# A hybrid decoder layer on one core: chunk 0's q projection by blocks of 128 input features, with other priorities and filler shares

## The chip, the cores and the metric

One core of a Trainium2 chip runs one launch of the kernel. The metric is the device time in microseconds (us). Before the change, three timed runs gave 1933.70, 1939.51 and 1939.64 us (median 1939.51).

## What is computed

One layer on x of 2048 rows by 1024 features, all in float32. The reference, cut to what matters:

```python
h = rms_norm(x, attn_norm_g[l])
z = h @ w_in[l]
# columns of z: q 512, k 128, v 128, gate_b 512, gate_c 512, xc 512
q = rms_norm(q, q_norm_g[l])
k = rms_norm(k, k_norm_g[l])
y_attn = swa_sink_attention(q, k, v, sinks[l])     # 8 heads, 2 kv heads, window 128
y_conv = gate_b * short_conv(gate_c * xc, conv_w[l])
y = jnp.concatenate([rms_norm(y_attn, attn_out_g[l]),
                     rms_norm(y_conv, conv_out_g[l])], axis=-1)
x = x + y @ w_out[l]
hm = rms_norm(x, mlp_norm_g[l])
x = x + jnp.square(jax.nn.relu(hm @ w_up[l])) @ w_down[l]
```

## The kernel before

**Products.** TensorE multiplies in fp32r. An operand is split into a high part (a cast, on ScalarE, ACT) and a low part (operand minus high part, on VectorE, DVE), and one product becomes three: high by high, high by low, low by high (`mm3`, L266 to L268). So every weight that is loaded is split first; splits are L458/L459 in the first chunk and L245/L246 elsewhere.

**Stages.** The mixers (input projection, attention, convolution, output projection) run over four chunks of 512 rows, each four tiles of 128 rows. Weights of the input and output projections are split in chunk 0, stored to DRAM (`keep`), and loaded as parts in chunks 1 to 3. Then follows the MLP, whose up and down projections use seven products instead of eight for each 2 by 2 blocking, 2688 matmuls each (L1427 up, L1534 down), with operands in the pools `op_x` and `wop`.

**The first chunk.** x comes as four row tiles (`x0_0` to `x0_3`, the first in two halves), and the q, k, v weights in pieces of 256 columns: pieces 0 and 1 are q, piece 2 is k and v. TensorE starts with idle products (`spin`, L511), turns a row tile with eight transposes (L468), ACT and VectorE move it out of PSUM with the norm's gain (L474, L476, 128x128 at a time), and `product0` (L488) multiplies it by piece 0, row tile by row tile: 24 matmuls of 256 columns for each. This part is under `manual_schedule`: every engine runs it as written. Pieces 1 and 2 follow in `project_qkv(0)`. The row statistics come from `norm_stats` (a square with a running sum, L275); z is scaled by them at the end. The x tiles stay in memory as chunk 0's residual.

**What sets the order elsewhere.** A scheduler orders instructions by priority; `ahead(i)` reads an offset from `PRIO[stage][i]`. `FILL` gives, for each attention step of a chunk, how many steps of the other work go behind it (convolution, the convolution half of the output projection, and the next chunk's norm, transposes L294 and q, k, v projection). Each engine runs its queue strictly in order. [...]

**Lines that the steps touch.** L282 scales an x tile of the next chunk by its row statistics, L294 transposes it, L298 and L299 move it out of PSUM as high and low part; L768 and L769 sum squares of the attention output, behind ACT's L767; L892 adds an output projection to the residual. At the MLP's start L396 loads operand pieces of the normed rows, L411 loads weights of the up projection, L416 and L417 split them, L899 stores x1 on GpSimd's (POOL) queue, and L1111 are memsets of POOL that take the first buffers of the MLP's pools.

Of the kernel before, what the change touches and what calls it, by code (L numbers as in the profile page):

```python
# [7 lines left out]
F32 = mybir.dt.float32  # L8
# [71 lines left out]
SPIN = (5, 3)  # L80
SOON = 300
# [21 lines left out]
def hymba_layer(  # L103
# [99 lines left out]
    n_pieces = [0]  # L203
# [232 lines left out]
    x0 = [row("x1", f"x0_{t}", NT) for t in range(NT)]  # L436
    z0 = [zrow(f"z0_{t}") for t in range(NT)]
    raw0, raw1 = (raw_part(f"raw_qkv{pc}") for pc in range(2))
    hl0, hl1 = (high_low(0, f"w_qkv{pc}") for pc in range(2))
# [9 lines left out]
    def load_x0(t, cut=1):  # L449
        for i in range(cut):  # L450
            r = slice(i * D // cut, (i + 1) * D // cut)
            nc.sync.dma_start(x0[t][:, r], xf[t * P : (t + 1) * P, r])

    load_w0 = lambda i: nc.sync.dma_start(*cols256(wi, 0, pieces=2)(raw0)[i])

    def split0(i, raw, hl):
        r = slice(i * 512, (i + 1) * 512)
        nc.scalar.copy(hl[0][:, r], raw[:, r])  # L458
        nc.vector.tensor_tensor(hl[1][:, r], raw[:, r], hl[0][:, r].bitcast(F32), op=ALU.subtract)  # L459

    def moved(t, part):

        for i in range(2):
            kk = i * (KD // 2)
            if not part:
                pts[t, i] = bank("at", f"pt_a0_{t}_{i}")
                for j in range(4):
                    nc.tensor.transpose(pts[t, i][:, j * P : (j + 1) * P], x0[t][:, (kk + j) * P : (kk + j + 1) * P], ident)  # L468
            else:
                p3 = pts.pop((t, i)).rearrange("p (k t) -> p k t", k=4)  # L470
                dh, dl = (d[:, kk : kk + 4, t * P : (t + 1) * P] for d in h)
                for k in range(KD // 2):
                    g = g_in[kk + k]
                    nc.scalar.activation(dh[:, k], p3[:, k], AF.Copy, scale=g)  # L474
                for k in range(KD // 2):
                    nc.vector.scalar_tensor_tensor(  # L476
                        dl[:, k], p3[:, k], g_in[kk + k], dh[:, k].bitcast(F32), op0=ALU.mult, op1=ALU.subtract
                    )

    w0 = [w.rearrange("p (k c) -> p k c", k=KD) for w in hl0]  # L480

    def product0(t, i, ks=range(KD)):

        if (i, ks[0]) == (0, 0):
            pzs[t] = bank("mm", f"pz0_0_{t}")[:, :256]
        a, b = ((0, 0), (1, 0), (0, 1))[i]
        for k in ks:
            nc.tensor.matmul(  # L488
                pzs[t], h[a][:, k, t * P : (t + 1) * P], w0[b][:, k, :], start=i + k == 0, stop=i + k == KD + 1
            )  # L490

    def put_z(t):
        nc.scalar.activation(z0[t][:, :256], pzs[t], AF.Copy, scale=rs0[:, t : t + 1])

    pts, pzs = {}, {}

    with tc.manual_schedule(engines={ET.PE, ET.Activation, ET.DVE, ET.Pool, ET.SP}):
        nc.scalar.dma_start(g_rows, attn_norm_g[0].rearrange("(k p) -> k p", p=P))
        nc.scalar.activation(warm, mhalf[:, :1], AF.Square)
        load_x0(0, cut=2)  # L500
        load_w0(0)
        load_w0(1)
        for t in range(1, NT):
            load_x0(t)
        nc.sync.dma_start(*cols256(wi, 256)(raw1)[0])

        idle = bank("mm", "idle")[:, :P]

        def spin(n):
            for _ in range(n):  # L510
                nc.tensor.matmul(idle, ident, ident, start=True, stop=True)  # L511
# [5 lines left out]
        moved(0, 0)  # L517
        moved(0, 1)
        spin(SPIN[1])
        for i in range(4):  # L520
            split0(i, raw0, hl0)
            product0(0, 0, range(2 * i, 2 * i + 2))
            if i == 1:
                moved(1, 0)
        product0(0, 1)
        product0(0, 2)
        for t in range(1, NT):
            moved(t, 1)
            for i in range(4 if t + 1 == NT else 0):
                split0(i, raw1, hl1)  # L530
            norm_stats(x0[t - 1], f"a0_{t - 1}", rs0[:, t - 1 : t])
            if t > 1:
                put_z(t - 2)
            if t + 1 < NT:
                moved(t + 1, 0)
            for i in range(3):
                product0(t, i)
        norm_stats(x0[NT - 1], f"a0_{NT - 1}", rs0[:, NT - 1 : NT])
        put_z(NT - 2)
        put_z(NT - 1)  # L540
        rs0_in = nc.gpsimd.tensor_tensor(rs0_2, rs0, rs0, op=ALU.mult).ins


    with tc.tile_pool(name="mix_small", bufs=1) as mix_small, tc.tile_pool(name="mix", bufs=1) as mix:
# [10 lines left out]
        def project_qkv(c, h, z):  # L555

            z += z0 if not c else [zrow(f"z{c}_{t}") for t in range(NT)]
            if not c:
                keep(hl0, "qkv0")
            if not c:  # L560
                keep(hl1, "qkv1")
                for pc in range(1, 3):
                    hl = weights(cols256(wi, pc * 256), c, f"qkv{pc}") if pc > 1 else hl1
                    w4 = [w.rearrange("p (k c) -> p k c", k=KD) for w in hl]
                    for t in range(NT):
                        ps = bank("mm", f"pz{c}_{pc}_{t}")[:, :256]
                        hk = lambda s, k, t=t: h[s][:, k, t * P : (t + 1) * P]
                        for k in range(KD):
                            mm3(ps, lambda s, k=k: hk(s, k), lambda s, k=k: w4[s][:, k, :], k == 0, k == KD - 1)
                            if k % 2 and k < KD - 1:  # L570
                                yield
                        z_in.append(
                            nc.scalar.activation(
                                z[t][:, pc * 256 : (pc + 1) * 256], ps, AF.Copy, scale=rs0[:, t : t + 1]
                            ).ins
                        )
                        yield
                return

            both = []  # L580
            for half in range(2):
                hl = high_low(c, f"w_q{half}_{c}")
                for i in range(2):
                    for pc in range(2):
                        nc.sync.dma_start(
                            hl[i].bitcast(F32).rearrange("p (k c) -> p k c", k=KD // 2)[:, :, pc * 256 : (pc + 1) * 256],
                            parts_dram[f"qkv{pc}"][i].rearrange("p (k c) -> p k c", k=KD)[
                                :, half * (KD // 2) : (half + 1) * (KD // 2)
                            ],
                        )  # L590
                both.append([w.rearrange("p (k c) -> p k c", k=KD // 2) for w in hl])
# [20 lines left out]
        z_in = []  # L612
# [328 lines left out]
        def besides(c, before, h, yt, rc, x1, h_next, z_next):  # L941
# [105 lines left out]
        z = []  # L1047
        for _ in project_qkv(0, h, z):
            pass
# [10 lines left out]
        g_qk = const.tile([P, 2, DH], F32, name="g_qk")  # L1060
        nc.sync.dma_start(g_qk[:, 0, :], q_norm_g[0].partition_broadcast(P))
        nc.sync.dma_start(g_qk[:, 1, :], k_norm_g[0].partition_broadcast(P))
        with tc.issue_after(rs0_in):
            nc.gpsimd.tensor_scalar(g_qk[:, 0, :], g_qk[:, 0, :], DH**-0.5, None, op0=ALU.mult)
        sink = const.tile([P, HEADS], F32, name="sink")
        nc.sync.dma_start(sink, sinks[0].partition_broadcast(P))
# [3 lines left out]
        cw = const.tile([P, NCT, 3], F32, name="cw")  # L1070
        for t in range(3):
            nc.sync.dma_start(cw[:, :, t], conv_w[0][t].rearrange("(i p) -> p i", p=P))

        g_cols = const.tile([P, KD], F32, name="g_cols")
        nc.sync.dma_start(g_cols, mlp_norm_g[0].rearrange("(k p) -> p k", p=P))
        g_y = const.tile([P, 2, NCT], F32, name="g_y")
        for kv in range(KVH):
# [496 lines left out]
```

## Time and profile before

| | |
|---|---|
| timed runs | 1933.70, 1939.51, 1939.64 us |
| profiled execution | 1936.33 us, span 1934.6 us, mean granted clock 0.999 |
| TensorE (PE) busy | 1916.7 us, 99% of the span, 9025 matmuls |
| weight loads (PEld) | 1596.0 us, beside the matmuls |
| VectorE (DVE), ScalarE (ACT), GpSimd (POOL) busy | 1206.7, 837.7, 273.3 us |
| DMA | 412.25 MB, mean 213 GB/s over the span |
| first product of the q projection | at 8.57 us |
| end of chunk 0's q, k, v projection | at 48.80 us |
| up projection, from its long unbroken run | from 735 us |
| down projection | from 1321.43 us to the end |

The profile is of one execution, 1936.33 us by itself, and the span starts and ends with the first and last recorded instruction. In a timeline row the first number is the start, the second the length; "idle before <- releaser" says how long the engine had waited and what ended that. PE is TensorE's matmul side; a busy time of PE contains pipelined ends, so the pace of a row of matmuls is better read from the start of one group to the start of the next. In a windows row the last three numbers are the granted clock of TensorE (1.00 is full), the share of the 16 DMA engines in use and GB/s.

### The profile page before, as it was taken

The page shows a single profiled execution, that of the slowest core. Times are in us where ns is not written, and L with a number is a line of the kernel's source. Part 1 is how long each engine was busy: PE and PEld are TensorE (multiplying, and loading weights), DVE is VectorE, ACT ScalarE, POOL GpSimd, SP SyncE. Part 2 cuts the span into 40 slices and gives each one's busy share as a digit, 9 for nine tenths or more (in the row PEclk, how much of TensorE's full clock was granted, in tenths as well). Part 3 has the DMA queues.
Part 4 walks back from the last instruction along what each step waited for, and adds up shares of the span by engine and source line. Part 5 has one row for each costly group of instructions (what it writes and reads, how often), then busy time and mean ns, then how long its engine had stood idle before and what let it go on. Part 6 is the DMA issues. An engine that isn't in the chain of part 4 may idle for free.

```text
span 1934.6 us, 24806 instructions
## 1 busy us (share of the span) xinstructions
PE 1916.7 (99%) x9025; PEld 1596.0 (82%) x9025; DVE 1206.7 (62%) x1872; ACT 837.7 (43%) x1593; POOL 273.3 (14%) x473
## 2 busy tenths in 40 slices
PE   9999999999999999999999999999999999999999
PEld 9888888888888788888877888888888888888887
DVE  4885667447556768899878766666534334448541
ACT  6563445345344437445465554554422333232220
POOL 1112203312221112222201111101000000100000
PEclk9999999999999999999999999999999999999999
DMA  9774855464474787877665544437964457776631
GB/s 324 274 261 150 288 223 188 169 255 155 163 276 170 241 299 277 250 216 249 227 222 191 180 162 143 164 123 295 376 218 151 143 163 229 262 229 219 211 135 55
DMA packets 240634, 412.25 MB, mean 213 GB/s; under 512 B 51704, under 2 KB 147968, under 8 KB 228736
## 3 DMA queue, kind: packets, MB, share of 16 engines
q1 hardware_dynamic: 211824, 335.15, 51.3%
q0 software_dynamic: 15424, 51.40, 6.8%
q10 hardware_dynamic: 13264, 24.13, 3.3%
q8 instruction: 71, 1.16, 0.2%
q14 instruction: 51, 0.42, 0.1%
HBM read 284.78 MB, written 125.83 MB: 212 GB/s over the span
## 4 chain that ended last, share of the span: by engine, by line
PE 84%; issue 5%; DVE 4%; DMA 4%; ACT 2%; POOL 1%; SPq 1%; ACTq 0%; POOLq 0%; DVEq 0%
PE d L1534 31%; PE u L1427 23%; PE pout L266 2%; PE pout L268 2%; PE pout L267 2%; PE pz L266 2%; PE pz L267 2%; PE pz L268 2%; PE pc_c L266 2%; PE px_c L266 2%; PE px_c L267 2%; PE px_c L268 2%; PE pc_c L268 2%; PE pc_c L267 2%; PE psc_b L665 1%
## 5 line engine op out<-in xcount | busy, mean ns | idle before, releaser
L1427 PE MATMUL u<-op_x,wop 128*128 128x512 f32 x2688 | 612.5, 390 | 3.0 <-DVE wop L417 1.3
L1534 PE MATMUL d<-op_w,op_f 128*128 128x512 f32 x2688 | 609.4, 389 | 0.0
L1427 PEld LDWEIGHTS u<-op_x,wop 128*128 128x128 f32 x2688 | 503.7, 188 | 111.4 <-DVE wop L417 4.0
L1534 PEld LDWEIGHTS d<-op_w,op_f 128*128 128x128 f32 x2688 | 504.7, 188 | 104.6
L398 DVE TENSOR_TENSOR op_f<-op_f 128x1024 fp32r<-128x1024 f32 x112 | 136.9, 1225 | 237.8 <-ACT op_f L397 237.4
L397 ACT CAST op_f<-op_f 128x1024 fp32r<-128x1024 f32 x112 | 118.0, 1054 | 355.9 <-DMA op_f<-fop 343.7
L416 ACT CAST wop<-wu 128x512 fp32r<-128x512 f32 x156 | 96.4, 621 | 92.0 <-PE u L1427 87.7
L417 DVE TENSOR_TENSOR wop<-wu,wop 128x512 fp32r<-128x512 f32 x156 | 111.7, 717 | 34.1 <-ACT wop L416 19.0
L1163 POOL DMA_DIRECT2D fop<-s x96 | 52.3, 545 | 433.3 <-DVE s L1166 426.4
L1169 DVE TENSOR_TENSOR u<-u,u 128x512 f32<-128x512 f32 x128 | 87.8, 686 | 18.8 <-PE u L1427 18.8
L398 DVE TENSOR_TENSOR op_w<-raw,op_w 128x1024 fp32r<-128x1024 f32 x56 | 68.4, 1222 | 25.4 <-ACT op_w L397 25.4
L397 ACT CAST op_w<-raw 128x1024 fp32r<-128x1024 f32 x56 | 58.9, 1053 | 42.3 <-PE d L1534 20.1
L1175 ACT ACTIVATE u<-u 128x512 f32<-128x512 f32 x64 | 40.6, 634 | 51.7 <-DVE u L1169 50.0
L682 ACT ACTIVATE sc_b<-sc_b,ngm_b 128x128 f32<-128x128 f32 x128 | 49.9, 392 | 26.5 <-DVE ngm_b L679 26.5
L714 POOL TENSOR_SCALAR_AFFINE_SELECT pp_b<-pp_b 128x512 fp32r<-128x512 f32 x60 | 41.1, 697 | 116.9 <-ACT pp_b L707 63.4
L1376 POOL DMA_DIRECT2D wds<-raw x16 | 8.6, 535 | 333.8 <-DVE raw L1374 333.8
L416 ACT CAST wop<-wu_s 128x512 fp32r<-128x512 f32 x64 | 39.5, 621 | 35.6 <-PE u L1427 27.4
L266 PE MATMUL pout<-w_wo,yt_c 128*128 128x512 f32 x128 | 52.4, 410 | 0.0
L268 PE MATMUL pout<-w_wo,yt_c 128*128 128x512 f32 x128 | 51.9, 406 | 0.0
L267 PE MATMUL pout<-w_wo,yt_c 128*128 128x512 f32 x128 | 51.2, 400 | 0.0
L266 PE MATMUL pout<-w_wo,at_b 128*128 128x512 f32 x128 | 50.2, 395 | 0.2 <-DVE x L892 0.2
L267 PE MATMUL pout<-w_wo,at_b 128*128 128x512 f32 x128 | 50.0, 391 | 0.3 <-DVE w_wo L249 0.3
(255 smaller groups left out, 3132.7 us busy)
## 6 DMA issues: line engine op xcount, KB each, us to landing
op_f<-fop SPq DMA_DIRECT2D x112, 512.0 KB, 4.5
raw<-in_w_down_dram SPq DMA_DIRECT2D x72, 512.0 KB, 4.4
wu<-in_w_up_dram SPq DMA_DIRECT2D x128, 256.0 KB, 3.8
w_wo<-wo SPq DMA_DIRECT2D x24, 1024.0 KB, 6.8
fop<-s POOLq DMA_DIRECT2D x96, 256.0 KB, 2.7
fop<-u ACTq DMA_DIRECT2D x64, 256.0 KB, 2.3
op_x<-xop SPq DMA_DIRECT2D x28, 512.0 KB, 6.5
w_q<-qkv SPq DMA_DIRECT2D x24, 512.0 KB, 6.0
```

The source lines that it names most:

```text
L266: nc.tensor.matmul(ps, st(0), mv(0), start=first, stop=False)
L267: nc.tensor.matmul(ps, st(0), mv(1), start=False, stop=False)
L268: nc.tensor.matmul(ps, st(1), mv(0), start=False, stop=last)
L397: nc.scalar.copy(op[:, 0], raw)
L398: nc.vector.tensor_tensor(op[:, 1], raw, op[:, 0].bitcast(F32), op=ALU.subtract)
L416: splits.append(nc.scalar.copy(hi, blk).ins)
L417: nc.vector.tensor_tensor(lo, blk, hi.bitcast(F32), op=ALU.subtract)
L682: nc.scalar.activation(sc[:, hd, :], sc[:, hd, :], AF.Exp, bias=ngm[:, hd : hd + 1], accum_out=den[:, hd : hd + 1])
L1163: eng.dma_start(fop_dram[tb][ORDER_DOWN.index(i)][n // 2][:, n % 2], b)
L1169: return nc.vector.tensor_tensor(dst, ps, b, op=ALU.add).ins
L1427: nc.tensor.matmul(pt, wops[i][:, a, k, :], xops[tb, p][k // 2][:, b, k % 2, :], start=p not in GOES_ON and k + j == 0, stop=k + j == NB + ...
L1534: nc.tensor.matmul(ps[tb][j], fs[tb][:, a, k, j * P : (j + 1) * P], w[:, b, k, :], start=first and p not in GOES_ON and k + n == 0, stop=l ...
```

## The change

1. **Loads.** x of chunk 0 comes by blocks of 128 features: one tile [128, 4, 1024] in a pool of its own ("first"), blocks 0 and 1 singly (512 rows by 512 B), the others in pairs. The q weights come by the same blocks of 128 input features with all 512 columns, block 0 on ACT's queue. The small loads of gains, sinks and convolution weights go behind them.
2. **Loop.** For each block k: split of the weights, four transposes into one PSUM bank, one move of 128x512 on ACT and one on VectorE, 12 matmuls of 512 columns into four banks that stay open over the eight blocks. Transposes of block k+2 stand behind the products of block k. The k, v piece is loaded at k = 3 and multiplied after the loop, still in the order as written.
3. **Spin.** The second group of three idle products goes (`SPIN`).
4. **Residual and weights later.** Chunk 0's residual is loaded from x again, after its last z (four times 512 KB). The q parts are stored as two halves by features, so chunks 1 to 3 load them with four transfers of 1 MB instead of eight of 512 KB.
5. **Tables.** `PRIO`, `FILL` and `SOON` change, and a memset takes the first buffer of the MLP's pool "w".

The core of the diff:

```diff
-SPIN = (5, 3)
-SOON = 300
+SPIN = (5, 0)
+SOON = 330
-    (40, 0, 160, -10, 10, 0, 80, 10, -20, 30, 0, 300),
+    (40, 0, 160, -10, 10, 0, 10, 60, -20, 30, 0, 300),
...
-    n_pieces = [0]
+    n_pieces = [2]
...
+        def load_x0(k, n):
+            r = slice(k * P, (k + n) * P)
+            nc.sync.dma_start(x0[:, :, r], xf[:CH, r].rearrange("(t p) c -> p t c", p=P))
...
+        def turn(k):
+            pts[k] = bank("at", f"pt_a0_{k}")
+            for t in range(NT):
+                nc.tensor.transpose(pts[k][:, t * P : (t + 1) * P], x0[:, t, k * P : (k + 1) * P], ident)
...
+        def product0(k, order):
+            for i, t in order:
+                a, b = ((0, 0), (0, 1), (1, 0))[i]
+                nc.tensor.matmul(
+                    pzs[t],
+                    h[a][:, k, t * P : (t + 1) * P],
+                    hl0[k][:, b],
+                    start=k + i == 0,
+                    stop=k + i == KD + 1,
+                )
...
+        load_w0(nc.scalar, 0, 1)
         nc.scalar.activation(warm, mhalf[:, :1], AF.Square)
+        load_x0(0, 1)
+        load_x0(1, 1)
+        load_w0(nc.sync, 1, 1)
+        for k in range(2, KD, 2):
+            load_x0(k, 2)
+            load_w0(nc.sync, k, 2)
+        load_gains(0)
...
+        turn(0)
         spin(SPIN[1])
+        turn(1)
+        for k in range(KD):
+            split0(k)
+            moved(k)
+            if k == KH - 1:
+                raw = raw_part("raw_qkv2")
+                nc.sync.dma_start(*cols256(wi, AW)(raw)[0])
+                load_gains(1)
+            if k >= KH:
+                norm_stats(x0[:, k - KH], f"a0_{k - KH}", rs0[:, k - KH : k - KH + 1])
+            if k + 1 < KD:
+                product0(k, [(i, t) for i in range(3) for t in range(NT)])
+            else:
+                product0(k, [(i, t) for t in range(NT) for i in range(3)])
+            if k + 2 < KD:
+                turn(k + 2)
...
-            x1 += [] if c else x0
-            for t in range(NT if c else 0):
+            for t in range(NT):
                 r = (c * NT + t) * P
                 xr = row("x1", f"x1_{c}_{t}", NT)
-                nc.sync.dma_start(xr, xf[r : r + P, :])
+                with nullcontext() if c else tc.issue_after(z_in[-1]):
+                    nc.sync.dma_start(xr, xf[r : r + P, :])
...
-    for tag in ("f12", "s1", "s2", "s4", "u4", "f11"):
+    for tag in ("f12", "s1", "s2", "s4", "u4", "f11", "w"):
         nc.gpsimd.memset(piece(tag, f"{tag}_first")[:, :1], 0.0)
```

The order of TensorE's queue at the start of the program, before (`pt_a` are transposed x tiles, `idle` the idle products, `pz` the accumulators of q, `h_a` and `w_qkv` the split operands):

```order
L515 MATMUL pg<-ident,g_rows 128x8
L468 MATMUL pt_a_0_0_276<-ident,x_0_236 128x128 x4
L468 MATMUL pt_a_0_1_281<-ident,x_0_236 128x128 x4
L511 MATMUL idle<-ident 128x128 x3
L488 MATMUL pz_0_0_307<-w_qkv_0_246,h_a_250 128x256 x4
L468 MATMUL pt_a_1_0_314<-ident,x_1_237 128x128 x4
L468 MATMUL pt_a_1_1_319<-ident,x_1_237 128x128 x4
L488 MATMUL pz_0_0_307<-w_qkv_0_246,h_a_250 128x256 x4
```

The same place after the change, from the transposes of block 0 to the first product of the low weights:

```order
L496 MATMUL pt_a_0_290<-ident,x_265 128x128 x4
L496 MATMUL pt_a_1_295<-ident,x_265 128x128 x4
L508 MATMUL pz_0_0_300<-w_q_0_242,h_a_250 128x512
L508 MATMUL pz_0_1_301<-w_q_0_242,h_a_250 128x512
L508 MATMUL pz_0_2_302<-w_q_0_242,h_a_250 128x512
L508 MATMUL pz_0_3_303<-w_q_0_242,h_a_250 128x512
L508 MATMUL pz_0_0_300<-w_q_0_242,h_a_250 128x512
```

The idle products between transposes and products are gone, and the first eight transposes are two blocks of 128 features of all four row tiles instead of one row tile.

VectorE's queue near the end of chunk 0's attention, before (`xt_a_2` is x tile 2 of chunk 1, `o_b` the attention output of the last row tile but one, `x_0` the residual):

```order
L768 TENSOR_TENSOR o_b_1712<-o_b_1712 128x256 [waits Activation_49]
L648 TENSOR_TENSOR kw<-ptk_b_1729,kw 64x128
L769 TENSOR_TENSOR o_b_1712<-o_b_1712 128x128 [waits DVE_49]
L299 TENSOR_TENSOR h_h_1562<-pt_a_1_4_1751,h_h_1561 128x4x128
L892 SCALAR_TENSOR_TENSOR x_0_236<-pout_1_1_0_1804,rc_808,x_0_236 128x512 [waits PE_49]
L282 SCALAR_TENSOR_TENSOR xt_a_2_1687<-xt_a_2_1687,rs_a_2_1692,g_attn 128x1024 [waits DMAHW5_49,Pool_49]
```

And after the change (lines L768 and L892 have become L782 and L906):

```order
L282 SCALAR_TENSOR_TENSOR xt_a_2_1549<-xt_a_2_1549,rs_a_2_1554,g_attn 128x1024 [waits DMAHW6_49,Pool_49]
L906 SCALAR_TENSOR_TENSOR x_0_0_1415<-pout_1_1_0_1666,rc_662,x_0_0_1415 128x512 [waits PE_49]
L780 TENSOR_TENSOR at_b_1579<-o_b_1574,at_b_1579 128x512 [waits Activation_49]
L690 COPY_PREDICATED sc_b_1687<-later,psc_b_0_1688 128x128 [waits Activation_49]
L299 TENSOR_TENSOR h_h_1424<-pt_a_2_0_1639,h_h_1423 128x4x128 [waits Activation_49]
L782 TENSOR_TENSOR o_b_1574<-o_b_1574 128x256 [waits Activation_49]
```

The scale of the x tile has moved from behind the sums of the attention output to ahead of them.

SP's queue at the start of the MLP, before (`op_x` are operand pieces, `wu` weights of the up projection):

```order
L396 DMA op_x_2_1_6973<-xop_1_77 128x1024 [waits DMAHW5_49,PE_49]
L411 DMA wu_12_6987<-in_w_up_dram 128x4x128 [waits DMAHW6_49]
L396 DMA op_x_6_0_6977<-xop_2_78 128x1024 [waits DMAHW7_49,Pool_49]
L396 DMA op_x_6_1_6981<-xop_2_78 128x1024 [waits DMAHW0_49,PE_49]
L411 DMA wu_12_6989<-in_w_up_dram 128x4x128 [waits DMAHW1_49]
```

And after the change (`xt_m_0` is the first row tile of x1 of the last chunk, stored by POOL's queue before, which is the semaphore DMASW1):

```order
L396 DMA op_x_2_1_6825<-xop_1_77 128x1024 [waits DMAHW3_49,PE_49]
L1219 DMA xt_m_0_7369<-x_dram 128x1024 [waits DMAHW4_49,DMASW1_49]
L396 DMA op_x_6_0_6829<-xop_2_78 128x1024 [waits DMAHW5_49,Pool_49]
L396 DMA op_x_6_1_6833<-xop_2_78 128x1024 [waits DMAHW7_49,DMAHW6_49,DVE_49]
L411 DMA wu_12_6839<-in_w_up_dram 128x4x128
```

The load of x1 stood 26 rows further down before, behind the weights of the up projection; it now stands ahead of `op_x_6_0` and of the first `wu_12`.

More of the change, by code (lines that the diff above doesn't have):

```diff
@@ L432, in begin_mlp @@
             wops[i] = split_up(b, f"{m}_{p}")
-    x0 = [row("x1", f"x0_{t}", NT) for t in range(NT)]
     z0 = [zrow(f"z0_{t}") for t in range(NT)]
-    raw0, raw1 = (raw_part(f"raw_qkv{pc}") for pc in range(2))
-    hl0, hl1 = (high_low(0, f"w_qkv{pc}") for pc in range(2))
+    raw0 = [raw_part(f"raw_q{half}") for half in range(2)]
+    hl0 = [wop_pool.tile([P, 2, AW], F32R, tag="wop", name=f"w_q0_{k}", bufs=NWOP) for k in range(NWOP)]
+    hl0 += [pool.tile([P, 2, AW], F32R, tag="at", name=f"w_q0_{k}", bufs=NAT) for k in range(NWOP, KD)]
     h = parts(pool, "h", "a0")
@@ L447, in hymba_layer @@
     g_in = [g_in_all[:, k : k + 1] for k in range(KD)]
[L449 to L478, printed above, removed]
@@ new lines, in first_chunk @@
+        for t in range(NT):
+            ps = bank("at", f"pz0_1_{t}")[:, :256]
+            hk = lambda s, k, t=t: h[s][:, k, t * P : (t + 1) * P]
+            for k in range(KD):
+                mm3(ps, lambda s, k=k: hk(s, k), lambda s, k=k: w4[s][:, k, :], k == 0, k == KD - 1)
+            z_in.append(nc.scalar.activation(z0[t][:, AW:], ps, AF.Copy, scale=rs0[:, t : t + 1]).ins)
+        return rs0_in, hl
+    z_in = []
+    with tc.tile_pool(name="first", bufs=1) as first:
+        with tc.manual_schedule(engines={ET.PE, ET.Activation, ET.DVE, ET.Pool, ET.SP}):
+            rs0_in, w_qkv2 = first_chunk(first)
@@ L544, in hymba_layer @@
+    keep(w_qkv2, "qkv2")
+    for half in range(2):
+        d = dram.tile([2, P, 2048], F32, name=f"q{half}")
+        parts_dram[f"q{half}"] = [d[i] for i in range(2)]
+        with tc.high_priority(offset=-LATER):
+            for k in range(KH):
+                nc.sync.dma_start(
+                    d[:, :, k * AW : (k + 1) * AW].rearrange("i p c -> p i c"), hl0[half * KH + k].bitcast(F32)
+                )
     with tc.tile_pool(name="mix_small", bufs=1) as mix_small, tc.tile_pool(name="mix", bufs=1) as mix:
@@ L555, in project_qkv @@
         def project_qkv(c, h, z):
[L557 to L591, printed above, removed]
+            z += [zrow(f"z{c}_{t}") for t in range(NT)]
+            both = [[by_k(w) for w in weights(None, c, f"q{half}")] for half in range(2)]
             w4 = [w.rearrange("p (k c) -> p k c", k=KD) for w in weights(None, c, "qkv2")]
```

111 lines of the change are left out of this document (49 added, 62 removed), and 10 rows, old and new, of tables (FILL, PRIO).

## The prediction

> **What bounds the kernel now.** I read the page first, then the waits of the matmul engine over the whole span, then the first 50 us as a timeline and as windows. The page has busy shares, and the chain that ended last:
>
> ```profile
> PE 1916.7 (99%) x9025; PEld 1596.0 (82%) x9025; DVE 1206.7 (62%) x1872; ACT 837.7 (43%) x1593; POOL 273.3 (14%) x473
> PE 84%; issue 5%; DVE 4%; DMA 4%; ACT 2%; POOL 1%; SPq 1%; ACTq 0%; POOLq 0%; DVEq 0%
> 1321.43 609.29 PE d L1534 x2688
> ```
>
> The last row is from the chain in order of time: 2688 products in 609.29 us, 226.7 ns each for 512 columns, without a gap. TensorE is the bound, and it is 18 us (1934.6 - 1916.7) short of never idle. So the change can win in three ways: fewer or wider matmuls, a full clock earlier, or less idling. The three longest waits of TensorE (total, times, longest, in us) are short each:
>
> ```profile
> PE pt_a L294 <- DVE h_h L299: 1.7, 5, 0.5
> PE idle L511 <- POOL ident L170: 1.6, 1, 1.6
> PE u L1427 <- DVE wop L417: 1.3, 3, 0.5
> ```
>
> The place with most to win is the start. TensorE's timeline there (start, length, idle before and what ended it), and then windows with the busy time of PE, PEld, DVE, ACT and POOL, the granted clock and the DMA share:
>
> ```profile
> 1.58 2.50 PE L511 MATMUL idle<-ident 128*128 128x128 f32 x10 [1.58 <-POOL ident L170]
> ...
> 4.22 1.97 PE L468 MATMUL pt_a<-ident,x 128*128 128x128 f32 x8
> 5.98 1.49 PE L511 MATMUL idle<-ident 128*128 128x128 f32 x6
> 8.57 1.02 PE L488 MATMUL pz<-w_qkv,h_a 128*128 128x256 f32 x4 [1.10 <-ACT w_qkv L458]
> 10.55 1.39 PE L468 MATMUL pt_a<-ident,x 128*128 128x128 f32 x8 [0.96 <-DMA x<-in_x_dram]
> ...
> 19.14 1.04 PE L468 MATMUL pt_a<-ident,x 128*128 128x128 f32 x8
> 19.93 5.99 PE L488 MATMUL pz<-w_qkv,h_a 128*128 128x256 f32 x48
> ```
>
> ```profile
> 0.00:7.79 7.79, 5.88 (x25) 5.34 (x25) 1.41 (x6) 3.67 (x10) 1.78 (x18) 1.00 0.68 222
> 7.79:11.20 3.41, 1.65 (x10) 1.25 (x11) 3.41 (x8) 2.28 (x4) 0.00 (x0) 1.00 1.03 411
> 11.20:14.61 3.41, 3.41 (x19) 3.41 (x17) 2.17 (x9) 3.22 (x10) 0.06 (x1) 0.50 1.05 315
> 14.61:25.76 11.15, 11.15 (x97) 11.15 (x96) 6.73 (x20) 9.57 (x27) 2.05 (x6) 1.00 0.72 203
> 25.76:48.80 23.04, 23.04 (x195) 23.04 (x193) 9.50 (x18) 12.05 (x26) 5.87 (x12) 1.00 1.04 408
> ```
>
> Three things are to be seen. The first product runs at 8.57 us, after waiting for split weights. Eight transposes take 1.76 us from 4.22 to 5.98, but 0.79 from 19.14 to 19.93 (0.10 each): TensorE is at half pace early, though the clock column says 1.00 there (I trust the pace). And the thin stretch 7.79 to 11.20 (1.65 us busy of 3.41) is followed by one with a granted clock of 0.50. The last row is the 192 products of the two later pieces, 120 ns each; the projection of chunk 0 ends at 48.80.
>
> **The change, part by part.**
>
> *q projection by feature blocks.* 192 products of 256 columns become 96 of 512: 192 x 0.120 = 23.0 us against 96 x 0.2267 = 21.8, so -1.3 us. The transposes stay 32. When does the first product run? The loads, splits and moves now:
>
> ```profile
> 0.80 0.59 ACTq L498 DMA_DIRECT2D g_rows<-in_attn_norm_g_dram  x1
> 0.81 0.86 SPq L452 DMA_DIRECT2D x<-in_x_dram  x2
> x<-in_x_dram SPq DMA_DIRECT2D x2, 256.0 KB, 3.2
> raw_qkv<-in_w_in_dram SPq DMA_DIRECT2D x2, 512.0 KB, 6.6
> L458 ACT CAST w_qkv<-raw_qkv 128x512 fp32r<-128x512 f32 x8 | 4.5, 645 | 0.6 <-DMA raw_qkv<-in_w_in_dram 0.6
> L1059 ACT COPY rs_row<-pr 128x512 f32<-128x512 f32 x1 | 0.6, 578 | 0.0
> L459 DVE TENSOR_TENSOR w_qkv<-raw_qkv,w_qkv 128x512 fp32r<-128x512 f32 x8 | 5.1, 687 | 0.0
> ```
>
> x block 0 is 256 KB like the half tile now loaded first, so it lands near 4.1. The weights of block 0 are 256 KB too (512 KB took 6.6), issued on ACT's queue near 1.4: they land between 4.6 and 6.0. Then ACT copies (0.57 unloaded, 0.645 mean) and moves (0.58, as the copy from PSUM): first product at 6.0 to 7.8, and I take 7.0. VectorE needs 0.69 for each of its two, 1.4 per block; ACT 1.2, from block 4 on 1.1 more for a norm's square. TensorE needs 12 x 0.227 + 4 x 0.10 = 3.1 us per block, so both engines keep ahead. So do loads: a block is 512 KB, and even the 222 GB/s of the first window bring one in 2.4 us. This is the cover of everything else in the loop; gone, each us of a late block is a us of time.
>
> From the first product: 21.8 + 24 x 0.10 = 24.2 us at full pace. The three idle products dropped (six rows of 0.21 at half pace) filled a wait, so they save nothing themselves, but they held TensorE busy before 7.79. Without them the stretch 4.37 to 7.79 has 8 transposes (1.76) and 0.8 of products: 2.5 of 3.41 us. That lies between the stretch that kept half clock behind it (1.65) and the one from 1.58 to 4.37 (2.8 busy, still half pace after it). So I take the half pace until 11.20, with (11.2 - 7.0)/2 = 2.1 us lost; the stretch after that is full in any case, since no wait for x tiles is left in it. The q part then ends at 7.0 + 24.2 + 2.1 = 33.3. The k and v piece is 96 x 0.12 = 11.5 us, to 44.8: **-4.0 us** against 48.80. The bounds: full pace from 7.79 gives 43.1 (-5.7); a first product at 7.8 with half pace to 14.61 gives 46.9 (-1.9).
>
> [...]
>
> *Other loads.* The k, v weights are issued inside the loop and land long before 33. The residual x of chunk 0 is loaded a second time: 2 MB at the rate of the next row is 6 us of all DMA engines, in a stretch that is nearly full:
>
> ```profile
> 60.00:80.00 20.00, 20.00 (x100) 16.69 (x99) 17.38 (x41) 11.97 (x38) 4.19 (x7) 1.00 0.95 327
> ```
>
> TensorE is never idle there, and the sums that read the residual come only at the out projection, after 120. I cost it at 0, and up to +2 if it pushes the x tiles of chunk 1, whose last wait is known (chain, then VectorE and TensorE):
>
> ```profile
> 137.61 5.93 DMA xt_a<-in_x_dram
> 145.34 0.43 DVE L768 TENSOR_TENSOR o_b<-o_b 128x256 f32<-128x256 f32 x1 [1.15 <-ACT o_b L767]
> 147.69 1.27 DVE L282 SCALAR_TENSOR_TENSOR xt_a<-xt_a,rs_a,g_attn 128x1024 f32<-128x1024 f32 x1
> 149.02 0.65 PE L294 MATMUL pt_a<-ident,xt_a 128*128 128x128 f32 x4 [1.13 <-DVE xt_a L282]
> ```
>
> Half the q weight loads (4 of 1 MB for 8 of 512 KB) frees four SP issues per chunk, and SP has time: 0.
>
> *Mixers' priorities.* In the order of VectorE, the scale of x tile 2 of chunk 1 (L282, at 147.69) now stands ahead of the attention sums that held it up (L768): TensorE's wait of 1.13 and the one of 0.6 around it should go, -1.9; one earlier wait grows as transposes come closer together, +1.0. Net **-0.9**. The other chunks' waits are of the same size and shift both ways; I take 0, with -3 to +2 as ends (all of the listed waits, or two of them more).
>
> *MLP's start.* A load of the x1 rows (xt_m) now stands on SP ahead of the operand pieces and first weights of the up projection, and waits for a store that POOL issues:
>
> ```profile
> 696.68 13.99 SPq L396 DMA_DIRECT2D op_x<-xop  x2
> 706.44 0.64 POOL L899 DMA_DIRECT2D x_dram<-x  x1 [14.70 <-DVE x L892]
> 720.87 0.19 POOL L1111 MEMSET s_first<- 128x1 f32 x3 [6.10 <-DMA x_dram<-x]
> 712.88 21.47 PE L1427 MATMUL u<-op_x,wop 128*128 128x512 f32 x94
> x_dram<-x SPq DMA_DIRECT2D x12, 512.0 KB, 3.5
> wu<-in_w_up_dram SPq DMA_DIRECT2D x128, 256.0 KB, 3.8
> ```
>
> SP stands still until 710.7 now as well. Such a store takes 3.5 us as a median, and the last one held POOL's memset for 6.1; at 5 for this one, SP goes on at 711.4; two operand loads and the weights are issued by 712.7, land at 716.5, are split by 717.9 (1.34 by the page's L416 and L417), and are wanted at 717.9, 22 products behind 712.88. I take **+0.5**, from 0 to +9. The memset for the dummy waits in POOL's row where others wait: 0.
>
> Sum: -4.0 - 0.9 + 0.5 = -4.4. The first wait (1.6 for the identity) stays. The profiled execution took 1936.33, so 1931.9; the three timed runs are 1933.70, 1939.51 and 1939.64 (with the profiled one 1937.3 in the mean), so the same program scatters by 3 us around my base. I put the forecast at **1932.0**.
>
> **The rivals.**
>
> *The clock is free early and the mixers gain.* For it: the phase of the stretches is not shown to be fixed, and the start of before had full pace from 7.79. Start -5.7, mixers -0.9 - 3: 1936.3 - 9.6 + 0.5 = 1927.
>
> *The start gains nothing that lasts.* SP and DMA are nearly full from 25 to 80, so TensorE could wait at the x tiles of chunk 1 for what it won before: with the DMA landing at 143.5 as the fixed point, 1936. Against it: TensorE waits little there, and the tile is loaded behind buffers that come free earlier too.
>
> *Slower: the up projection's first weights come late.* The mechanism is the blocked SP row above. Its point is a store that lands after 711.4: beyond it each us is a us of time. If the slot is freed only with the last store (720.8, by POOL's memset row), the weights are issued at 722.1, landed at 725.9 and split at 727.3, against 717.9: +9.4, so 1931.4 + 9.4 = 1941. For it: SP runs strictly in order, and the row before had let those loads out at 696. Against it: the row names the first of four stores.
>
> *The loads starve the blocks,* because x now comes in pieces of 512 B to 1 KB. It needs blocks slower than 3.1 us (170 GB/s); at 5 us each the q part ends at 47: start +9.7, 1946. The 222 GB/s speak against it.
>
> **How the numbers follow.** Forecast 0.50, early clock with mixers 0.25, nothing that lasts 0.11, late weights 0.11, starved blocks 0.03. A measurement of this kernel can tell 0.3% (5.8 us) from no change: below 1930.5 is faster. The early clock case lies there (0.25), and of the forecast's own spread (1928 to 1936, by the bounds of the start and the other terms) two fifths of its 0.50, so 0.20: together 0.45 faster. Slower by 0.3% needs 1942: 0.03 and half of the late weights, 0.09 with some of the forecast's own upper end. The rest, 0.46, is within. The range from 1924 (both early cases with all waits) to 1940 leaves out most of the two slow cases.
>
> **What would show it.** Right: first product near 7.0, k and v done near 45, half pace ended at 11.2; no wait of TensorE at x tile 2 near 145; no wait longer than 1 us at the up projection's second operand. Wrong: waits on DMA or ACT inside the eight blocks, a second thin stretch with clock 0.50, or TensorE idle for several us behind SP near 715.

## The result, and the profile after

The changed kernel takes 1933.67 us (median of 21 runs, 1930.90 to 1936.15) against 1937.02 (21 runs, 1931.94 to 1941.29) before: ratio 0.9982, 95% interval 0.9976 to 0.9988, so 3.4 us less. The forecast was 1932.0. The profiled execution took 1934.50 us, 1.8 less than the one before. The page (busy, and shares of the chain) still has TensorE as the bound:

```profile
PE 1913.2 (99%) x8923; PEld 1589.5 (82%) x8923; DVE 1204.1 (62%) x1848; ACT 830.8 (43%) x1565; POOL 275.9 (14%) x474
PE 93%; DMA 2%; DVE 2%; issue 1%; POOL 1%; ACT 1%; SPq 0%; ACTq 0%; POOLq 0%; DVEq 0%
```

TensorE's timeline at the start, then its first work behind the k and v piece (`pr`), and the first transpose of the normed q (`ptq_b`, which reads `z`):

```profile
4.22 1.91 PE L496 MATMUL pt_a<-ident,x 128*128 128x128 f32 x8
6.43 3.02 PE L508 MATMUL pz<-w_q,h_a 128*128 128x512 f32 x12 [0.29 <-ACT h_a L500]
9.29 0.60 PE L496 MATMUL pt_a<-ident,x 128*128 128x128 f32 x4
...
42.81 0.60 PE L1070 MATMUL pr<-ident,rs_row 128*128 128x128 f32 x4
...
47.11 0.45 PE L652 MATMUL ptq_b<-ident,z 128*128 128x128 f32 x1 [3.01 <-DVE z L641]
```

The first product runs at 6.43, and its 12 products take 2.86 us to the next transposes: full pace from the first one (the next blocks take the same 2.86). The projection ends at 42.81 against 48.80, so 6.0 us are won. The last row shows 3.0 of them lost again in one wait. TensorE's longest waits in the whole span (total, times, longest; before, none was over 1.7 in total) are for split weights of the up projection (`wop`), for `z`, and for x1 rows loaded back for the MLP's norm (`xt_m`):

```profile
PE u L1421 <- ACT wop L416: 4.6, 1, 4.6
PE ptq_b L652 <- DVE z L641: 3.0, 1, 3.0
PE pt_m L308 <- DVE xt_m L282: 2.6, 3, 1.8
```

The windows around the two new waits (busy PE, PEld, DVE, ACT, POOL, granted clock, DMA share, GB/s):

```profile
42.81:47.11 4.30, 1.30 (x9) 0.84 (x8) 2.02 (x5) 1.44 (x4) 2.67 (x3) 0.95 1.01 350
47.11:50.53 3.42, 3.42 (x12) 2.61 (x13) 1.19 (x5) 2.54 (x6) 2.29 (x2) 0.57 1.02 413
50.53:53.94 3.41, 3.41 (x17) 2.80 (x16) 2.31 (x4) 2.98 (x9) 0.90 (x2) 1.00 1.02 425
714.46:719.04 4.58, 0.16 (x1) 0.00 (x0) 2.45 (x2) 1.85 (x3) 0.00 (x0) 1.00 1.07 379
719.20:722.60 3.40, 3.40 (x8) 2.68 (x9) 2.78 (x5) 2.60 (x5) 0.00 (x0) 0.51 1.15 345
```

Each wait is paid twice: behind the empty stretch comes one of 3.4 us with a granted clock of 0.57 or 0.51, which costs about 1.5 and 1.7 us more. So the wait at 47 costs 4.6 us, the one at 714 about 6.3.

Where the 6.0 us stay is read from marks that stand in both traces. From the chain and the timelines, before and after: the scores of the second row tile (16 matmuls) 65.67 and 64.25, those of chunk 2 390.16 and 386.96, the first store of x1 in the last chunk 706.44 and 703.02, the down projection's start 1321.43 and 1319.52. The lead is 6.0 us at 43, 1.4 at 65, 3.2 at 390, 3.4 at 705 and 1.9 at the end. The matmuls behind the projection of chunk 0 are the same in both kernels; taken where equally much of that work is still to come, the lead is the same at the last four marks.

### The profile page after: what moved, and what is told of

It is laid out like the page before. It is cut to its first block, busy times and chain, and to the rows that moved or that the text cites. A ratio compares the mean times of both kernels' runs of the same rounds, so it can differ in the third digit from the quotient of the medians.

```text
span 1932.8 us, 24559 instructions
## 1 busy us (share of the span) xinstructions
PE 1913.2 (99%) x8923; PEld 1589.5 (82%) x8923; DVE 1204.1 (62%) x1848; ACT 830.8 (43%) x1565; POOL 275.9 (14%) x474
## 4 chain that ended last, share of the span: by engine, by line
PE 93%; DMA 2%; DVE 2%; issue 1%; POOL 1%; ACT 1%; SPq 0%; ACTq 0%; POOLq 0%; DVEq 0%
PE d L1528 32%; PE u L1421 31%; PE pout L266 2%; PE pout L268 2%; PE pout L267 2%; PE pz L266 2%; PE pz L267 2%; PE pz L268 2%; PE psc_b L679 2%; PE pc_c L266 2%; PE px_c L266 2%; PE px_c L267 2%; PE pc_c L267 2%; PE pc_c L268 2%; PE px_c L268 2%; PE pb_c L267 1%
## 5 line engine op out<-in xcount | busy, mean ns | idle before, releaser
L417 DVE TENSOR_TENSOR wop<-wu_s,wop 128x512 fp32r<-128x512 f32 x64 | 45.0, 702 | 12.4 <-ACT wop L416 12.1
L266 PE MATMUL pout<-w_wo,at_b 128*128 128x512 f32 x128 | 50.2, 395 | 0.0
```

Of the source, the lines that this page charges most:

```text
L266: nc.tensor.matmul(ps, st(0), mv(0), start=first, stop=False)
L417: nc.vector.tensor_tensor(lo, blk, hi.bitcast(F32), op=ALU.subtract)
```

## The experiments

Ratios are to the kernel before, timed on the same chip; the changed kernel has 0.9982. The intervals in brackets are about 0.0009 either way, 1.7 us. "The dummy" is the memset that takes the first buffer of the MLP's pool "w".

### 1. Without the dummy

```diff
-    for tag in ("f12", "s1", "s2", "s4", "u4", "f11", "w"):
+    for tag in ("f12", "s1", "s2", "s4", "u4", "f11"):
```

> The changed kernel without the memset on the first buffer of the MLP's pool w. In SP's order the load of x1 (xt_m) then stands 30 rows further down again, and the first weights of the up projection ahead of it. Theory (the dummy moves the load, and that makes TensorE's wait of 4.6 us at L1421): that wait goes. If the dummy has no other effect, 4 us less than the changed kernel (1929.5); if it is also what removed the 4.2 us of small stalls that the kernel before has between 735 and 1100, those come back and the time stays at 1933 to 1934. Rival (the weights land late because the DMA engines are full): the wait stays at 4 us or more, wherever the load stands.

Measured: 1936.80 us, ratio 1.0003 (0.9994 to 1.0012): the whole gain is gone. The wait is 3.0 instead of 4.6 and begins 1.7 us later, and the stalls between 735 and 1100 are back. That stretch as a window, of the kernel before, the changed one, and this one:

```profile
735.00:1100.00 365.00, 363.12 (x1592) 298.24 (x1593) 311.39 (x449) 200.25 (x331) 73.85 (x104) 1.00 0.70 224
```
```profile
735.00:1100.00 365.00, 365.00 (x1612) 302.24 (x1611) 312.76 (x451) 203.02 (x334) 79.05 (x106) 1.00 0.71 225
```
```profile
735.00:1100.00 365.00, 363.78 (x1596) 298.43 (x1596) 310.65 (x450) 199.15 (x331) 74.43 (x105) 1.00 0.70 224
```

TensorE is never idle there in the changed kernel; without the dummy it loses 16 matmuls' time in the window, and the kernel before lost 20. Most of the stalls stand between 1000 and 1040. Neither theory was whole: the dummy does move the load of x1, and its stalls do come back, but the wait at the MLP's start does not go either. Without the dummy the first weights stand ahead on SP (SyncE, whose queue issues these loads), and wait there themselves for a buffer that TensorE's output projection frees (a wait of 14.7 us on SP): SP issues them at 708.6.

```profile
708.62 0.38 SPq L411 DMA_DIRECT2D wu<-in_w_up_dram  x1
```

So beside the changed kernel the dummy is worth 4 us.

### 2. The small loads on GpSimd

```diff
-                load_gains(1)
...
         rs0_in = nc.gpsimd.tensor_tensor(rs0_2, rs0, rs0, op=ALU.mult).ins
+        load_gains(1)       # its seven loads by nc.gpsimd
```

> The changed kernel with its seven small loads (cw, g_cols, g_y) issued by GpSimd after the row statistics instead of by SP inside the loop. Theory (TensorE's wait of 3.0 us for z at 47 us comes from ACT's split of w_wc, which stands ahead of z and waits for a load that SP issued only at 29.3 behind the small loads): the load of w_wc is issued near 26, lands near 35, the wait of 3.0 goes, and with it the slow pace of the 3.4 us behind it (1.5): 4 to 4.5 us less than the changed kernel, near 1929.5. Rival (the DMA engines are full between 25 and 45, so the weights land near 38 in any order): no change, 1933.5.

Measured: 1931.43 us, ratio 0.9980 (0.9971 to 0.9989), not to be told from the changed kernel. The profiled execution shows no wait for z, but its projection ended 1.6 us later, at 44.39, which hides it. The load of w_wc was issued at 27.36 and the split began at 36.11, against 29.32 and 38.47.

### 3. Both edits

Edits 1 and 2 in one kernel.

> Both edits in one kernel: small loads on GpSimd, and no dummy. Theory: the two effects add, 1925 to 1929.5 (the lower end if the dummy costs its whole 4.6 us). Rivals: 1933.5 if neither place is what it seems.

Measured: 1933.15 us, ratio 0.9981 (0.9972 to 0.9990). Its rows judge edit 2 better, since the projection ended at 42.91 as in the changed kernel:

```profile
25.87 0.37 SPq L239 DMA_DIRECT2D raw_wc<-in_w_in_dram  x1
```
```profile
37.55 2.19 ACT L245 CAST w_wc<-raw_wc 128x512 fp32r<-128x512 f32 x4 [5.21 <-DMA raw_wc<-in_w_in_dram]
```
```profile
46.20 0.45 PE L652 MATMUL ptq_b<-ident,z 128*128 128x128 f32 x1 [1.99 <-DVE z L641]
```

Issued 3.5 us earlier, w_wc lands 0.9 us earlier, and TensorE still waits 2.0 us for z. That is the rival of experiment 2 for the larger part, though the two rows are not of one load alone: with edit 2, SP also issues the first residual load of x (512 KB) ahead of w_wc, at 24.55 and 23.07 in experiments 2 and 3, where it stood at 70.92. How much of the delay is that load is not shown.

The two effects do not add (1925 to 1929.5 was expected). Experiments 2 and 3 differ by the dummy alone, and their ratios, 0.9980 and 0.9981, do not: with edit 2 the dummy is worth nothing that can be told. So the 4 us of experiment 1 hold for that kernel and are not the dummy's own.

### 4. The dummy alone in the kernel before

```diff
-    for tag in ("f12", "s1", "s2", "s4", "u4", "f11"):
+    for tag in ("f12", "s1", "s2", "s4", "u4", "f11", "w"):
```

> The kernel before with the dummy alone. SP's order at the MLP's start becomes that of the changed kernel. Theory: TensorE waits 4 to 5 us for the first weights of the up projection; the time is 4 us above the kernel before if that is all, or equal to it within 1 us if the dummy also removes the 4.2 us of stalls between 735 and 1100. Rival (the dummy does nothing by itself and the order is from the tables): SP's order of before, no wait over 1 us, no change.

Measured: 1938.60 us, ratio 1.0014 (1.0005 to 1.0023). TensorE's timeline has the wait, and the window has no idle time:

```profile
720.53 79.68 PE L1427 MATMUL u<-op_x,wop 128*128 128x512 f32 x342 [4.35 <-ACT wop L416]
```
```profile
735.00:1100.00 365.00, 364.98 (x1610) 301.99 (x1609) 312.38 (x451) 203.47 (x334) 79.14 (x106) 1.00 0.70 225
```

The memset of one column alone makes both: the wait at the MLP's start and the stretch without stalls behind it. In the kernel before it costs 2.7 us net, where the first piece of the weights and its operand had been loaded from 696; in the changed kernel, where SP can issue them only at 708.6 without it, it gains 4. That this difference makes the sign is argued from the rows, and no run shows it by itself.

### 5. Row tile 0's chain ahead of the split of w_wc

```diff
+        behind = ExitStack()
+        if name == "wc0" and not c:
+            for ins in normed[0]:    # ACT's square, VectorE's last product of z
+                behind.enter_context(tc.issue_after(ins))
-        with ahead(7):
+        with ahead(7), behind:
...
```

> The changed kernel with the split of w_wc placed behind row tile 0's own chain: on ACT behind the square for the norm of q and k, on VectorE behind the last multiplication of z. Theory (ACT and VectorE run in order, so z of row tile 0, whose products end at 34, waits for weights that land at 38): the transposes of q start at 43.2 without the wait of 3.0, and without the slow pace of the next 3.4 us (1.4): 4 us less than the changed kernel, near 1929.5. Rival (w_wc is itself late, so its products wait in place of the transposes): a wait at pc_c of 2 us or more, and at most 1 us gained.

Measured: 1933.21 us, ratio 0.9982 (0.9974 to 0.9991). The wait for z and the low clock behind it are gone, as the two windows show:

```profile
42.80:47.10 4.30, 4.30 (x27) 3.63 (x26) 2.07 (x7) 0.74 (x1) 2.42 (x2) 1.00 0.82 294
47.10:50.50 3.40, 3.40 (x16) 2.80 (x15) 2.78 (x5) 3.32 (x7) 1.85 (x2) 1.00 0.91 285
```

So the cause of the wait at 47 is shown. But the time is the same: in the last chunk TensorE now waits for x1 tiles that are loaded back, and the first products behind the longest of these waits start 0.42 to 0.43 us apart (669.46 to 670.74) where those ahead of it start 0.23 apart.

```profile
PE pt_m L312 <- DVE xt_m L286: 4.2, 3, 3.4
```
```profile
659.46 7.16 DMA xt_m<-x_dram
```

The same load, the fourth of five behind 640, took 5.32 us in the changed kernel, and the 3.4 us of wait were 1.8 there. What is won early is partly lost at the transfers of the last chunk.

### 6. The up projection's weights ahead, the load of x1 behind

```diff
+            with tc.high_priority(offset=600) if n < START and x == a12 else nullcontext():
-            wts.setdefault(n, Weights(n, later=False)).piece(*x)
+                wts.setdefault(n, Weights(n, later=False)).piece(*x)
...
+            with tc.issue_after(ups[-1]):     # the last weight load so far, on SP
-            nc.sync.dma_start(xt, x1_dram[r : r + P, :])
+                nc.sync.dma_start(xt, x1_dram[r : r + P, :])
```

> The changed kernel (dummy kept) with the first four weights of the up projection's second operand issued ahead of the third operand's pieces, and the load of x1 behind them. Theory (the wait of 4.6 us at the MLP's start comes from SP's place for these loads): they are issued near 694, land by 705, the wait and the slow pace behind it (together 6 us) go, and the 4 us of stalls between 735 and 1100 stay away: 5 to 6 us less than the changed kernel, near 1928. Rival (the DMA engines bring no more in that time, so something else of the first products comes late instead): 0 to 2 us less, 1931.5 to 1933.5.

Measured: 1942.45 us, ratio 1.0030 (1.0018 to 1.0042): 9 us more than the changed kernel, which neither theory had. The wait at 714 is gone and stands 20 us later, and the stalls of 735 to 1100 are back:

```profile
735.31 43.20 PE L1423 MATMUL u<-op_x,wop 128*128 128x512 f32 x182 [3.59 <-ACT wop L416]
```
```profile
735.00:1100.00 365.00, 362.22 (x1576) 295.83 (x1577) 308.44 (x445) 197.12 (x327) 72.77 (x102) 1.00 0.70 221
```

In the profile the whole loss lies behind the MLP's start: the first store of x1 runs 0.4 us earlier than in the changed kernel (702.62), the down projection starts 6.3 later (1325.79). With experiments 1 and 4 this looks as if the early load of x1 were the half of the dummy's work that pays. Experiment 11 speaks against it: there x1 is loaded early, at 704.46, and between 1000 and 1100 TensorE runs 434 matmuls, against 443 in the changed kernel and 426 in the kernel before, so about half of the stalls are back. What the dummy does to remove them stays open.

### 7. Experiments 5 and 6 together

> Both edits in one kernel. Theory: the two places are 650 us apart and add up, 9 to 10 us less than the changed kernel, near 1924; faster than both kernels. Rival (what is won at 47 is lost at the next load that the chunks wait for): as the kernel with the weights alone, near 1928.

Measured: 1940.45 us, ratio 1.0020 (1.0010 to 1.0029), with a wait of 4.58 that ends at 732.42. Beside experiment 6 the median is 2 us lower, but the two intervals overlap. The rival holds better than the theory of 9 to 10 us less: the two edits do not add, and here the up projection waits another 3.6 us for split weights, in four places.

### 8. The changed kernel with the old tables

```diff
-SOON = 330
+SOON = 300
-    (40, 0, 160, -10, 10, 0, 10, 60, -20, 30, 0, 300),
+    (40, 0, 160, -10, 10, 0, 80, 10, -20, 30, 0, 300),
...
```

> The changed kernel with PRIO, FILL and SOON of the kernel before (SPIN and the dummy stay). Theory (the tables are worth what the stalls of the chunks show: about 1.3 us between 128 and 150 and 1.7 between 400 and 500, less what they cost between 500 and 690): 1 to 3 us more than the changed kernel, 1935 to 1937. Rival (the tables do nothing by themselves and the stall at 145 went with the earlier start): within 1 us of the changed kernel, 1933.5.

Measured: 1941.46 us, ratio 1.0023 (1.0013 to 1.0033): 8 us more than the changed kernel, where 1 to 3 were expected, and 4.5 more than the kernel before: the new start without its tables loses time. The profiled execution (1938.55, the lowest of its runs) is 4.1 us longer than that of the changed kernel. It starts slowly, which the tables do not touch:

```profile
6.79 1.12 PE L496 MATMUL pt_a<-ident,x 128*128 128x128 f32 x4 [1.46 <-DMA x<-in_x_dram]
7.58 5.49 PE L508 MATMUL pz<-w_q,h_a 128*128 128x512 f32 x12
12.86 0.65 PE L496 MATMUL pt_a<-ident,x 128*128 128x128 f32 x4
```

But it has no wait for z, and its second row tile's scores run 1.0 us earlier than in the changed kernel, so the 4.1 us do not come from the start. The first store of x1 runs 2.95 us later (705.97), so the tables are worth 3.9 between these marks; another 1.1 goes behind the MLP's start. Its waits at the chunks' ends (L294 for sums of squares 2.6 in all, for h 2.3) are 0.2 each in the changed kernel. That the tables matter is shown; the full size of 8 us is not explained by the one profile.

### 9. The new tables in the kernel before

The reverse of the diff of experiment 8, in the kernel before.

> The kernel before with PRIO, FILL and SOON of the changed kernel (SPIN stays, no dummy). Theory (the tables fit the changed start: they were worth 8 us there, but what they order depends on when the first chunk's pieces come): the same time as the kernel before or slower, 1936 to 1940. Rival (the tables alone are worth what they were in the changed kernel): 4 to 8 us less than the kernel before, 1929 to 1933.

Measured: 1935.29 us, ratio 0.9990 (0.9981 to 0.9998), 1.9 us less: between the theory and the rival. In the profiles, the tables gain 1.0 us between the second row tile's scores and the first store of x1, against 3.9 in experiment 8. Some of what they bring does not need the new start, but most of it does.

### 10. Six more idle products in the kernel before

```diff
-SPIN = (5, 3)
+SPIN = (5, 5, 4)
...
             if i == 1:
+                spin(SPIN[2])
                 moved(1, 0)
```

> The kernel before with six more idle products (counted as instructions in the code): two behind the first transposes, four behind the first four products, where TensorE waits in any case. Theory (the half clock from 11.2 to 14.6 comes from the thin stretch before it): that stretch is at full pace, 1.7 us less than the kernel before, 1935. Rival (the pace of the first microseconds is not set by how busy TensorE was): half pace as before, and no gain or 0.5 us lost, 1936.5 to 1937.

Measured: 1934.38 us, ratio 0.9983 (0.9974 to 0.9991): as much as the whole change. The windows of the start:

```profile
7.79:11.20 3.41, 2.57 (x18) 2.18 (x19) 3.34 (x7) 2.28 (x4) 0.00 (x0) 1.00 1.02 411
11.20:14.61 3.41, 3.41 (x31) 3.41 (x30) 2.17 (x9) 3.33 (x11) 0.09 (x1) 1.00 1.08 333
```

With 2.57 us of TensorE's work in the stretch to 11.20 instead of 1.65, the clock of the next is 1.00 instead of 0.50, and it holds 31 matmuls instead of 19. One profile would not show that the idle products did this: the profile of experiment 4, which has the start of the kernel before, has no half clock from 11.2 either (20 products from 10.60 in 2.48 us, 0.12 each). The timed runs show it: their mean granted clock is 0.9997 (11 runs) against 0.9984 (27 runs of the kernel before), which is 2.5 us of 1935. The theory holds for the mechanism.

### 11. The weights ahead of the operand pieces, with x1 early

Experiment 6 without its second part.

> The changed kernel (dummy and early load of x1 kept) with the four weights of the up projection's second operand ahead of the third operand's two pieces, behind the load of x1. Theory (in the changed kernel the weights took 11 us to land because 1 MB of operand pieces was issued just ahead of them): they land in 4 to 6 us, the wait of 4.6 shrinks to under 1, and the third operand, wanted 11 us later, is in time: 4 to 6 us less than the changed kernel, 1928 to 1929.5. Rival (the loads of this stretch have to move in any order, and the next one waits instead): another wait of 3 to 5 us within 30 us behind it, 1932 to 1934.

Measured: 1936.94 us, ratio 1.0000 (0.9991 to 1.0009). The rival is right about the wait, which stands 16 us later with the same length; the time is 3 us above its range.

```profile
734.93 65.30 PE L1422 MATMUL u<-op_x,wop 128*128 128x512 f32 x280 [4.44 <-ACT wop L416]
```

This execution also began slowly (12 products from 6.71 to 11.64). Four kernels with four orders of SP (the changed one, experiments 6, 7, 11) have one wait of 3.6 to 4.6 us between 714 and 736, and none of these orders removed it. In the kernel before no single wait there is over 0.9.

### 12. Experiments 2 and 5 together

> The changed kernel with the small loads on GpSimd and with row tile 0's chain ahead of the split of w_wc. Theory (both edits remove the same wait for z at 47): as the better one of them, 1931 to 1932. Rival (they remove different waits): their gains add, 1930.5 or less.

Measured: 1931.06 us, ratio 0.9964 (0.9952 to 0.9977), the lowest median of this study, 6 us below the kernel before, from five runs. The down projection starts at 1313.78, against 1319.52 in the changed kernel. Each edit alone gave nothing that can be told from the changed kernel, and together 3.5 us, with intervals that just touch. In the profile neither the wait for z nor the long one for x1's tiles is there; the wait at the MLP's start stays:

```profile
PE u L1426 <- ACT wop L420: 4.3, 1, 4.3
PE idle L536 <- POOL ident L170: 1.6, 1, 1.6
PE po_b L772 <- POOL pp_b L733: 1.4, 2, 0.9
PE pt_m L312 <- DVE xt_m L286: 0.9, 2, 0.6
```

Why the x1 tiles come in time here and not in experiment 5 was not tried.

## Why the prediction was right, point by point

- **Start: -4.0 forecast, -6.0 measured at 42.81.** The first product at 6.43 lies in the range of 6.0 to 7.8; the blocks never waited for a load or a split, so the cover held. The term that was mis-sized is the clock: 2.1 us were taken for a half pace until 11.20, and it cost nothing. The working took the stretches of the kernel before, which end at 7.79 and 11.20, as given. They are not: in this execution the transposes start 0.21 us apart up to 4.91 and 0.11 apart behind 5.75, and full clock begins at 5.70, ahead of the first product. In the other nine profiles with this start the first 12 products took 2.8 to 2.9 us in six, and 4.2 (experiment 2), 5.3 (8) and 4.9 (11) in three. Experiment 11 ran the case that was forecast:

```profile
5.64 1.12 PE L496 MATMUL pt_a<-ident,x 128*128 128x128 f32 x4 [0.30 <-DMA x<-in_x_dram]
6.71 5.09 PE L508 MATMUL pz<-w_q,h_a 128*128 128x512 f32 x12
11.64 0.60 PE L496 MATMUL pt_a<-ident,x 128*128 128x128 f32 x4
```

Its products start 0.43 us apart until 11.15 and 0.23 apart behind 12.3, and its projection ends at 45.16, where the forecast had 44.8. So the working holds for one of two outcomes, the less frequent one; that the profiled execution had the other was luck. No run puts the dropped idle products back, so whether they would have ended the half pace earlier in those three is not known.

- **Other loads: 0 forecast.** This step failed, though the sum came out. It asked only whether the k, v weights and x come in time, not what stands behind them on ACT and VectorE: the split of w_wc, waiting for weights issued at 29.32 behind the small loads (25.55 in the kernel before), stood ahead of z. The cost was 4.6 us with the clock (experiment 5). The rival "nothing that lasts" had named x tiles as the place; it was z.
- **Mixers: -0.9 forecast for chunk 0, 0 for the others; -2.0 measured.** The wait of 1.13 at x tile 2 is 0.20 after, as forecast, and the lead grows by 1.8 from 65 to 390 and 0.2 from there to 705. Beside the new start the tables are worth about twice that (3.9 in the profile of experiment 8).
- **MLP's start: +0.5 forecast, to +9; +1.5 measured.** The blocked SP row was there, and the store's landing near (SP went on at 706.05 behind a store of 3.0 us). From 700 to 706 the DMA engines' share was 0.25, where the kernel before had 0.89. The first weights then took 11.13 us to land instead of 3.8, behind 1 MB of operand pieces and beside the load and the stores of x1; this size was wrong, and the wait of 4.6 plus its clock is 6.3. But the stalls between 735 and 1100 went, which experiments 1 and 4 tie to the dummy and the prediction had at 0: the lead falls only by 1.5 from 705 to 1321.
- **Sum.** -6.0 + 4.6 - 1.8 - 0.2 + 1.5 = -1.9 in the profiled executions, -3.4 in the medians, -4.4 forecast. Of the signs of being wrong that the prediction named, two came: a second stretch at low clock (0.57 behind 47) and TensorE idle for several us behind SP near 715. A start that won 2 us more, a wait of 4.6 that was not in the sum and a gain that was not in it either made a time near the forecast; that they cancel was luck.

## What to carry to other kernels

A stretch ahead of the bound's first work is worth watching for the clock as much as for the work: idle products where TensorE waits in any case gained as much here as the whole change, and the new start with the old tables gained nothing. Ask of each wait that goes which in-order queue is now early for a load that is late, and count what follows an idle stretch at low clock as a part of its price (1.5 and 1.7 us behind the two here). One profile has one place where the clock changes (full from 7.79 us in the one of before, from 5.70 in the one after); a term that hangs on it needs both outcomes in the sum. What a table of priorities or a memset that takes a buffer is worth changes with the kernel around it: the same memset gained 4 us in one kernel, nothing in another, and lost 2.7 in a third.

## What the runs showed of the hardware

- In the changed kernel's trace full clock begins at 5.70 us. Half clock begins at 46.66 and at 719.09, and lasts 3.41 us both times; in the kernel before it lasts 3.41 us from 11.20. Ahead of 5.70 the trace has no clock record, and the column shows 1.00 there though the transposes start 0.21 us apart (0.11 at full pace). In the kernel before the records begin at 7.79, with full clock.
- Between 4.22 and 7.79 the kernel before ran eight transposes (1.76 us) and six idle products (0.21 us apart). In experiment 12 the 12 products that follow eight transposes (4.22 to 6.32) run at full pace from their first (2.88 us).
- An idle stretch of 3.0 us (at 47) or 4.6 us (at 719) is followed by 3.4 us at a granted clock of 0.57 or 0.51. A stretch of 3.41 us with 1.65 us busy (kernel before, 7.79 to 11.20) had half clock behind it, and with 2.57 us busy in these same 3.41 us (experiment 10) full clock followed. It took no long gap: none in the first was over 1.10 us. In experiment 9 half pace followed gaps of 0.97 us up to 8.11 and 0.91 up to 10.04 (eight transposes from there took 1.62 us to the next product, 0.79 at full pace).
- Two executions of the same code at the start differ by up to 2.4 us in the first 12 products (2.86 and 5.28), by when the half pace ends.
- With the DMA engines' share at 1.00 (changed kernel, 29.32 to 38.47), a load issued 3.5 us earlier landed 0.9 us earlier (experiment 3), with 512 KB more ahead of it.
